# Neighbourhood attention and rotary on one core: bias rows from memory, earlier rotary tables, gate per head

## The chip, the core and the metric

The kernel is one program on one NeuronCore of a Trainium2 chip. TensorE (PE) multiplies matrices and transposes, VectorE (DVE), ScalarE (ACT) and GpSimd (POOL) work element by element, SyncE (SP) issues DMAs, and ACT issues DMAs too, between its own operations. The metric is the device time of one execution in microseconds (us), lower is better. Where the text says head 4, the attention heads are counted from 0.

## The reference, cut to what matters

One layer, 2048 latent tokens on a 32 x 64 grid, 256 context tokens, width 1024:

```python
na_q, na_k, na_v, na_g, r_q, r_k, r_v, r_g = split(rmsnorm_modulated(x) @ w_in)   # and the same for the context
# group A, 8 heads of 64: each query sees an 8 x 16 window of keys, clamped to the grid, and all 256 context keys
s_loc = (q . k_window) * 64**-0.5 + na_rpb[h, dr + 7, dc + 15]     # masked outside of the window
s_ctx = (q . k_ctx) * 64**-0.5
y_na = softmax([s_loc, s_ctx]) @ [v_window, v_ctx] * silu(na_g)
# group B, 4 heads of 128: rotary on r_q and r_k, retention in both directions
y_ret = head_rmsnorm(retention(rotary(r_q), rotary(r_k), r_v)) * silu(r_g)
out = final_rmsnorm(x + gate * (concat(y_na, y_ret) @ w_out))
```

## The kernel before, in words

All matrix products of the projections are made of three terms of a value split into a high and a low part (`hhi`, `hlo` of the activations, `whi`, `wlo` of the weights), so one projection unit is 24 matmuls for 512 columns (`tform`, L351) or 48 for 256 columns (`tokform`, L362). The program has these stages, one after the other in time: preparation and projections up to about 562 us of the span, the attention of group A from 562 to about 1062 us, the rest of the projections and the backward pass of the retention to about 1145 us, and the forward pass of the retention with the output projection to the end. The schedule is manual: every engine executes its instructions in the order in which the Python code emits them.

The attention loop (`for t in range(NT + 3)`, L957) has 16 tiles of 128 queries per head, four row groups `i` of four column tiles `j`, 128 tiles in all. In the pass for tile t it emits the scores of tile t (`s_mm`, PE into PSUM tile `sS`), the normalization of tile t-1 (`s_norm`, L771 on POOL), the pass `s_min` of tile t (L760 on DVE: scores plus a bias row from `nb`, written to `sp`, with the running minimum), the transposes of tile t-2 (`p_tr`, PE, copied by ACT to `pt`, the low part by DVE in `p_lo`), and the product with v of tile t-3 (`pv`), after every second tile `combine`. Between these it calls `fill`, which takes 2 or 3 steps per tile from a generator with the leftover projection units of group B (`u_rv`, `u_rk`, `u_rq`: 8 steps per unit). So PE always has projection matmuls between the attention's own. Engines keep to this order strictly: a DVE instruction of a rotary unit that waits holds back the next `s_min` behind it, and PE cannot write the next `sS` before `s_min` has read the last.

The bias. `s_min` adds a row per query: -(relative position bias) inside the window and a huge number outside of it. The queries are scaled by -0.125, so the sum is the negated score, and the minimum is the softmax's shift. Three row types by three column types of tiles are needed per head. POOL builds the rows (`bias`, L724): from a slab of 16 x 32 values per query (`rpbe`, one load per head) and two small masks it makes `ep` once per row type (L730) and the rows in `nb0` or `nb1` per column type (L733): 12 POOL instructions per head. Edge types 0 and 2 share `nb0`, type 1 has `nb1`.

The loads. SP issues all loads of the stage, in program order: per head the keys `k` (twice 576 KB), the context values `vc`, eight groups of values `vt` of four pieces each (`load_v`, a ring of six groups), the queries `q` of a row group in two halves (`load_q`, a ring of two, asked for when the row group before begins), the gate `gt` (`load_gate`, one buffer), and from `fill` the weights `st`, the activations `hhi`, `hlo` of blocks 2 and 3 that were put aside in memory (`hS`, 16 loads of 512 KB), and the rotary tables. A DMA also waits for the landing of one issued eight or nine places before it in the common order of SP and ACT, whose semaphore it takes over.

Rotary. `u_rq` and `u_rk` load their table inside their own unit (`mid`: after step 3 of 8, or step 2), into the ring `t0` of two buffers, and DVE uses it when the unit's matmuls are done (L412 to L414, L448 and L450), then POOL adds (L415, L451).

The gate. Head pairs share a tile `y2` of 128 partitions: the even head fills partitions 0 to 63, the odd head 64 to 127, and after the odd head's row group POOL multiplies all 128 partitions by `gt` (L825) and ACT stores the tile to `yS`.

Of the kernel before, what the change touches and what calls it, by code (L numbers as in the profile page):

```python
# [18 lines left out]
P = 128  # L19
# [5 lines left out]
GW = 64  # L25
# [11 lines left out]
EROW0 = [4, 0, 0, 0]  # L37
ECOL0 = [8, 0, 0, 0]
# [32 lines left out]
]  # L71
RTYPE = [0, 1, 1, 2]
# [4 lines left out]
def hybrid_kernel(ctx: ExitStack, tc: tile.TileContext, a: dict, out: bass.AP):  # L77
# [290 lines left out]
    def mid(g, n, fn):  # L368
        for m in range(KC):
            next(g)  # L370
            if m == n:
                fn()
            yield
        return (yield from g)

# [24 lines left out]

    def u_rq(w, c0, ct, b):
        def load():
            for key in ("rot_c", "rot_s"):
                rot[key] = op.tile([P, 512], F32, name="t0")
                nc.sync.dma_start(rot[key], a[key][:, b * 512:(b + 1) * 512])

        g = tform(w, ct, b)
        pm, n, tok = yield from mid(g, 3, load) if ct == 0 else g
        rc, rs = rot["rot_c"], rot["rot_s"]
# [22 lines left out]
    def u_rk(w, c0, tp):  # L432
        def load():
            rot["k"] = op.tile([P, 2, 2, P], F32, name="t0")
            nc.sync.dma_start(rot["k"], a["rot_k"][tp * 256:(tp + 1) * 256].rearrange("(t p) s d -> p t s d", p=P))

        g = tokform(w, tp)
        pm = yield from mid(g, 2, load) if tp < 8 else g
        rt = rot.get("k")
# [59 lines left out]
    wseq = [(c0, -0.125 if us[0][0] is u_q else None) for c0, us in jobs[1:]] + [(c0, None) for _, c0 in fseq]  # L499
# [127 lines left out]
    def fill_stream(w):  # L627
# [72 lines left out]
    def load_e(hd, h):  # L700
        hd["e"] = kp.tile([P, 16, 32], F32, name="rpbe", bufs=1)
        nc.sync.dma_start(hd["e"], a["rpb_e"][h])

# [15 lines left out]
    mrow = mp.tile([P, 3, 16], F32, name="mrow")  # L719
    nc.sync.dma_start(mrow, a["na_rows"])  # L720
    mcol = mp.tile([P, 3, 32], F32, name="mcol")
    nc.sync.dma_start(mcol, a["na_cols"])

    def bias(hd, rt, ct):  # L724
        i, j = (0, 1, 3)[rt], (0, 1, 3)[ct]
        kr, cw = KWIN[i][1], CWIN[j][1]
        er, ec = EROW0[i], ECOL0[j]
        if ct == 0:
            hd["ep"] = mp.tile([P, kr, 32], F32, name="ep")
            nc.gpsimd.tensor_tensor(hd["ep"], hd["e"][:, er:er + kr, :],  # L730
                                    mrow[:, rt, er:er + kr].unsqueeze(2).to_broadcast([P, kr, 32]), ALU.subtract)
        t, o = nbz[int(rt == 1)], nbt[int(rt == 1), ct]
        nc.gpsimd.tensor_tensor(t[:, o:o + kr * cw].rearrange("p (a b) -> p a b", b=cw),  # L733
                                mcol[:, ct, ec:ec + cw].unsqueeze(1).to_broadcast([P, kr, cw]),
                                hd["ep"][:, :, ec:ec + cw], ALU.subtract)
# [19 lines left out]
    def s_min(t):  # L755
        h, i, j = dims(t)[:3]
        T = tl_st[t]
        n, big = T["nk"] + LC, int(RTYPE[i] == 1)
        o = nbt[big, CTYPE[j]] - T["lo"]
        nc.vector.tensor_tensor_reduce(T["sp"][:, :n], T["s"], nbz[big][:, o:o + n], 1.0, 3e38, ALU.add, ALU.min, T["st"][:, 0:1])  # L760
# [29 lines left out]
    def pv(t):  # L790
        h, i, j, kr0, kr, kc0, cw = dims(t)
        T, hd = tl_st[t], heads[h]
        pt, ng_, cn = T["pt"], T["ng"], 4 * cw
        if t % 2 == 0:
            tl_st["po"] = psc.tile([P, 2, 2, P], F32, name="po")
        po = tl_st["po"]
        for g in range(ng_):
# [6 lines left out]

    def load_gate(t):
        h, i = dims(t)[:2]
        gts[t // 4] = ap_.tile([P, 512], F32, name="gt", bufs=1)
        nc.sync.dma_start(gts[t // 4], gS[h // 2][:, i * 512:(i + 1) * 512])
# [540 lines left out]
```

## Time and profile before

| | |
|---|---|
| median of 3 runs | 1423.2 us (1421.59 to 1423.46) |
| the profiled execution, its own time | 1420.85 us |
| its span, first to last instruction | 1419.1 us |
| PE busy / DVE / ACT / POOL | 1351.0 / 641.2 / 530.7 / 560.1 us |
| mean granted PE clock | 0.986 |
| DMA, mean | 178 GB/s, 253.19 MB moved |

Times in the profile are counted from the span's start. A busy PE is not a PE at its best rate: the rows of a matmul overlap with the next, and at a lower granted clock (PEclk) the same matmul takes longer. In timeline rows the columns are start, duration, engine, line, operation, output <- inputs, and in brackets the idle time before it on that engine and what ended it. In the queue's rows (SPq) the duration is that of the issue with its wait.

### The profile page before, as it was taken

How to read it: one execution, taken by the hardware profiler on the slowest of the kernel's cores; microseconds unless marked ns; L12 is line 12 of the kernel's file. 1: busy time of each engine (PE TensorE's matmuls, PEld its weight loads, DVE VectorE, ACT ScalarE, POOL GpSimd, SP SyncE). 2: the span in 40 equal slices, each digit the busy share in tenths (PEclk: the TensorE clock that was granted, in tenths of full speed). 3: DMA queues.
4: the chain of work that ended last, by engine and by line, in shares of the span. 5: the costliest groups of instructions: out<-in, count | busy, mean ns of one | idle time of the engine just before them, and what ended most of it. 6: DMA issues, size and time to landing. Idle time of an engine off the chain costs nothing.

```text
span 1419.1 us, 22560 instructions
## 1 busy us (share of the span) xinstructions
PE 1351.0 (95%) x8380; PEld 1181.2 (83%) x8380; DVE 641.2 (45%) x1244; ACT 530.7 (37%) x1155; POOL 560.1 (39%) x579
## 2 busy tenths in 40 slices
PE   6989999999999999999999998898999989999997
PEld 2567899988887887998799888797999879888886
DVE  5786111100021221467766766575663634345445
ACT  5454212212212221555455444354562234333332
POOL 4442302112201221565655644375453155454442
PEclk9999999999999999999999999999999999999999
DMA  9444656223254676556666685757346998555433
GB/s 318 158 164 143 215 207 230 104 97 105 96 157 159 195 276 202 127 156 166 180 157 162 182 243 190 200 153 181 108 125 208 283 297 260 191 170 173 154 120 126
DMA packets 203631, 253.19 MB, mean 178 GB/s; under 512 B 13057, under 2 KB 151425, under 8 KB 202498
## 3 DMA queue, kind: packets, MB, share of 16 engines
q1 hardware_dynamic: 168098, 186.98, 45.2%
q10 hardware_dynamic: 35424, 64.76, 12.5%
q8 instruction: 67, 1.10, 0.3%
q14 instruction: 42, 0.34, 0.1%
HBM read 168.86 MB, written 82.84 MB: 177 GB/s over the span
## 4 chain that ended last, share of the span: by engine, by line
PE 73%; DMA 9%; DVE 6%; issue 3%; POOL 3%; ACT 2%; SPq 2%; DVEq 0%; POOLq 0%; ACTq 0%
PE mm L351 25%; PE mm L362 18%; PE mm L1192 11%; PE sS L751 3%; PE tr L778 2%; PE po L798 2%; PE mm L915 2%; DMA k<-kS 2%; PE tr L780 1%; DMA q<-qS 1%; PE po L800 1%; PE mm L295 1%; PE mm L1104 1%; PE mm L1103 1%; PE mm L1102 1%
## 5 line engine op out<-in xcount | busy, mean ns | idle before, releaser
L351 PE MATMUL mm<-hhi,whi 128*128 128x512 f32 x640 | 260.5, 407 | 0.0
L351 PE MATMUL mm<-hlo,whi 128*128 128x512 f32 x640 | 254.2, 397 | 4.8 <-DVE hlo L264 1.9
L351 PE MATMUL mm<-hhi,wlo 128*128 128x512 f32 x640 | 254.4, 397 | 0.2 <-DVE wlo L332 0.2
L362 PE MATMUL mm<-whi,hhi 128*128 128x256 f32 x768 | 225.5, 294 | 0.0
L362 PE MATMUL mm<-wlo,hhi 128*128 128x256 f32 x768 | 217.7, 283 | 2.5 <-POOL wlo L332 2.5
L362 PE MATMUL mm<-whi,hlo 128*128 128x256 f32 x768 | 217.2, 283 | 0.0
L332 POOL TENSOR_TENSOR wlo<-st,whi 128x256 fp32r<-128x256 f32 (+1 forms) x97 | 111.7, 1171 | 232.7 <-ACT whi L330 232.2
L782 ACT CAST pt<-tr 128x640 fp32r<-128x640 f32 (+1 forms) x128 | 95.6, 747 | 205.4 <-PE tr L780 193.0
L788 DVE TENSOR_TENSOR pt<-tr,pt 128x640 fp32r<-128x640 f32 (+1 forms) x128 | 113.9, 890 | 102.8 <-ACT pt L782 102.1
L362 PEld LDWEIGHTS mm<-wlo,hhi 128*128 128x128 f32 x768 | 146.0, 190 | 3.2 <-POOL wlo L332 3.1
L351 PEld LDWEIGHTS mm<-hlo,whi 128*128 128x128 f32 x640 | 121.4, 190 | 30.1 <-issue 2.5
L362 PEld LDWEIGHTS mm<-whi,hhi 128*128 128x128 f32 x768 | 146.3, 190 | 0.0
L362 PEld LDWEIGHTS mm<-whi,hlo 128*128 128x128 f32 x768 | 146.2, 190 | 0.0
L351 PEld LDWEIGHTS mm<-hhi,wlo 128*128 128x128 f32 x640 | 121.0, 189 | 29.4 <-DVE wlo L332 0.6
L351 PEld LDWEIGHTS mm<-hhi,whi 128*128 128x128 f32 x640 | 121.3, 190 | 28.7 <-issue 4.6
L771 POOL TENSOR_SCALAR sp<-sp,stt 128x640 f32<-128x640 f32 (+2 forms) x128 | 103.4, 809 | 100.7 <-DVE stt L770 79.8
L760 DVE CUSTOM_DVE_ANT_0 sp<-sS,nb 128x640 f32<-128x640 f32 (+2 forms) x128 | 105.5, 825 | 26.4 <-PE sS L751 20.3
L765 ACT ACTIVATE sp<-sp,stt 128x640 f32<-128x640 f32 (+2 forms) x128 | 107.4, 839 | 26.5 <-DVE stt L760 26.0
L751 PE MATMUL sS<-k,q 128*128 128x256 f32 (+3 forms) x512 | 100.6, 319 | 16.9 <-DVE stt L760 13.0
L751 PEld LDWEIGHTS sS<-k,q 128*128 128x128 f32 x512 | 84.5, 191 | 24.4 <-DVE stt L760 15.9
L1192 PE MATMUL mm<-wor,y 128*128 128x512 f32 x384 | 95.4, 397 | 1.0 <-DVE xt L1201 0.9
L1192 PE MATMUL mm<-won,y 128*128 128x512 f32 x336 | 89.9, 406 | 0.0
(216 smaller groups left out, 2307.5 us busy)
## 6 DMA issues: line engine op xcount, KB each, us to landing
st<-in_w_in_dram SPq DMA_DIRECT2D x48, 512.0 KB
q<-qS SPq DMA_DIRECT2D x64, 256.0 KB
vS<-o ACTq DMA_DIRECT2D x18, 512.0 KB
k<-kS SPq DMA_DIRECT2D x16, 576.0 KB
kS<-o SPq DMA_DIRECT2D x16, 512.0 KB
woS<-g ACTq DMA_DIRECT2D x32, 256.0 KB
qS<-o ACTq DMA_DIRECT2D x16, 512.0 KB
vt<-vS SPq DMA_DIRECT2D x128, 64.0 KB
```

The lines of the kernel that those rows point to most:

```text
L332: eng.tensor_tensor(l, r, f(h), ALU.subtract)
L351: nc.tensor.matmul(pm[:, :n], ww[:, k, cs], h[:, k, :], start=(k == 0 and i == 0), stop=(k == KC - 1 and i == 2))
L362: nc.tensor.matmul(pm[:, t * WG:(t + 1) * WG], h[:, k, o:o + P], ww[:, k, :], start=(k == 0 and i == 0), stop=(k == KC - 1 and i == 2))
L751: nc.tensor.matmul(o, hd["q"][i][:, hl, j * P:(j + 1) * P], k, start=(hl == 0), stop=(hl == 1))
L760: nc.vector.tensor_tensor_reduce(T["sp"][:, :n], T["s"], nbz[big][:, o:o + n], 1.0, 3e38, ALU.add, ALU.min, T["st"][:, 0:1])
L765: nc.scalar.activation(sp[:, :n], sp[:, :n], AF.Exp, bias=st[:, 0:1], scale=-1.0, accum_out=st[:, 1:2])
L771: nc.gpsimd.tensor_scalar(sp[:, :n], sp[:, :n], st[:, 2:3], 0.0, ALU.mult, ALU.add)
L778: nc.tensor.transpose(tr[:cn, g, :], sp[:, T["lo"] + g * cn:T["lo"] + (g + 1) * cn], ident)
L782: nc.scalar.copy(pt[:, :ng_ + 2, 0, :], tr[:, :ng_ + 2, :])
L788: nc.vector.tensor_tensor(pt[:, :n, 1, :], tr[:, :n, :], f(pt)[:, :n, 0, :], ALU.subtract)
L798: nc.tensor.matmul(po[:, t % 2, :, :], hd["vt"][kr0 // 4 + g][:cn, j, :], pt[:cn, g, :, :], start=(g == 0), stop=False)
L1192: nc.tensor.matmul(pm, yy[:, k, :], ww[:, k, sl], start=(k == 0 and i == 0), stop=(k == 3 and i == 2))
```

## The change

Four things are changed, and their places in the order of the loop:

- The host lays out the finished rows of bias and mask for each head and each of the nine tile types (`_bias_rows`, 3200 values per query and head, `rpb_t`). `bias` is now one DMA on SP per tile type straight into `nb0` or `nb1`: nine per head, of 128 rows of 288, 384 or 512 values (1152 to 2048 bytes). The slab, the masks, and the 96 POOL instructions are gone.
- The queries are scaled by +0.125, the rows hold the bias itself with a huge negative number outside, and the pass of `s_min` multiplies by -1.0 where it multiplied by 1.0.
- The rotary tables move to a ring of three (`rot` in the pool of `st`) and are asked for at step 2 of the unit before the one that uses them. Where a `u_rq` unit follows a `u_rq` unit, only the first of its two tables is, and the second at the start of its own unit.
- The gate is applied per head: `gt` of 64 partitions is loaded for each row group of every head, at j = 1 instead of j = 3 and into a ring of two, POOL multiplies 64 partitions after each row group (32 multiplications where there were 16), and ACT stores 64 partitions (32 stores where there were 16). The bytes are the same.
- `load_v` asks for value groups 3 and 4 one tile earlier.

```diff
+BT = [[(KWIN[i][1] * CWIN[j][1], 0, 0) for j in (0, 1, 3)] for i in (0, 1, 3)]
...
     def u_rq(w, c0, ct, b):
-        def load():
-            for key in ("rot_c", "rot_s"):
-                rot[key] = op.tile([P, 512], F32, name="t0")
-                nc.sync.dma_start(rot[key], a[key][:, b * 512:(b + 1) * 512])
-        g = tform(w, ct, b)
-        pm, n, tok = yield from mid(g, 3, load) if ct == 0 else g
+        pm, n, tok = yield from tform(w, ct, b)
+        rc, rs = rot["rot_c", b], rot["rot_s", b]
...
         def steps(g):
-            for v in g:
+            n = at[0]
+            at[0] += 1
+            is_rq = lambda k: k >= 0 and order[k][0] is u_rq
+            if is_rq(n - 1):
+                for e in needs(n)[1:]:
+                    rot_load(*e)
+            for m, v in enumerate(g):
+                if m == 2:
+                    for e in needs(n + 1)[:1 if is_rq(n) else 2]:
+                        rot_load(*e)
...
-    def bias(hd, rt, ct):
-        i, j = (0, 1, 3)[rt], (0, 1, 3)[ct]
-        kr, cw = KWIN[i][1], CWIN[j][1]
-        er, ec = EROW0[i], ECOL0[j]
-        if ct == 0:
-            hd["ep"] = mp.tile([P, kr, 32], F32, name="ep")
-            nc.gpsimd.tensor_tensor(hd["ep"], hd["e"][:, er:er + kr, :],
-                                    mrow[:, rt, er:er + kr].unsqueeze(2).to_broadcast([P, kr, 32]), ALU.subtract)
-        t, o = nbz[int(rt == 1)], nbt[int(rt == 1), ct]
-        nc.gpsimd.tensor_tensor(t[:, o:o + kr * cw].rearrange("p (a b) -> p a b", b=cw),
-                                mcol[:, ct, ec:ec + cw].unsqueeze(1).to_broadcast([P, kr, cw]),
-                                hd["ep"][:, :, ec:ec + cw], ALU.subtract)
+    def bias(h, rt, ct):
+        n, o = BT[rt][ct]
+        nc.sync.dma_start(nbz[int(rt == 1)][:, nbt[int(rt == 1), ct]:][:, :n], a["rpb_t"][h, :, o:o + n])
...
-        nc.vector.tensor_tensor_reduce(T["sp"][:, :n], T["s"], nbz[big][:, o:o + n], 1.0, 3e38, ALU.add, ALU.min, T["st"][:, 0:1])
+        nc.vector.tensor_tensor_reduce(T["sp"][:, :n], T["s"], nbz[big][:, o:o + n], -1.0, 3e38, ALU.add, ALU.min, T["st"][:, 0:1])
...
-        if h % 2 == 1 and jp == 1:
-            gt, y2 = gts.pop(t // 4), ys[i]
-            nc.gpsimd.tensor_tensor(y2, y2, gt, ALU.mult)
-            y_put(h // 2, i // 2, (i % 2) * 512, y2, 2)
+        if jp == 1:
+            gt = gts.pop(t // 4)
+            nc.gpsimd.tensor_tensor(y2[fin], y2[fin], gt[fin], ALU.mult)
+            store(yS[i // 2][h // 2, fin, (i % 2) * 512:(i % 2) * 512 + 512], y2[fin], 2)
...
-        if h % 2 == 1 and j == 3:
+        if j == 1:
             load_gate(t)
...
-        for g in {(0, 3): (3,), (1, 0): (4,), (1, 1): (5,), (1, 3): (6,), (2, 3): (7,)}.get((i, j), ()):
+        for g in {(0, 2): (3,), (0, 3): (4,), (1, 1): (5,), (1, 3): (6,), (2, 3): (7,)}.get((i, j), ()):
...
                 if j == 0:
                     load_q(nh, h + 1, 0)
-                    bias(nh, 0, 0)
+                    bias(h + 1, 0, 0)
                     load_v(nh, (0,))
```

PE's and DVE's instructions keep their order and number. Three places show what moves.

POOL, first tiles of head 0 (`wlo` is the low part of weights that the leftover units use, `sp` the scores of a tile, L771 their normalization), before:

```order
L332 TENSOR_TENSOR wlo<-st,whi 128x256 x2
L730 TENSOR_TENSOR ep<-rpbe,mrow 128x512
L733 TENSOR_TENSOR nb_3987<-mcol,ep 128x384
L771 TENSOR_SCALAR sp<-sp,stt 128x544
L332 TENSOR_TENSOR wlo<-st,whi 128x256 x2
L733 TENSOR_TENSOR nb_3987<-mcol,ep 128x512
L771 TENSOR_SCALAR sp<-sp,stt 128x640
```

The same place in the changed kernel, where the normalization is L768:

```order
L336 TENSOR_TENSOR wlo<-st,whi 128x256 x2
L768 TENSOR_SCALAR sp<-sp,stt 128x544
L336 TENSOR_TENSOR wlo<-st,whi 128x256 x2
L768 TENSOR_SCALAR sp<-sp,stt 128x640
L336 TENSOR_TENSOR wlo<-st,whi 128x256 x3
```

The two bias instructions that stood ahead of each first normalization of a row type are gone.

SP, head 4, from the end of its first reload of `hS` to the queries of its row group 3 (the `q` in the last row but one of the first list), before:

```order
L684 DMA hhi<-hS_0_85 128x1024
L435 DMA t_7514<-in_rot_k_dram 128x2x256
L684 DMA hlo<-hS_1_86 128x1024
L694 DMA k_7532<-kS_63 64x2304 x2
L697 DMA vc<-vS_66 128x2x128
L716 DMA vt<-vS_66 96x1x128
L716 DMA vt<-vS_66 128x1x128 x2
L716 DMA vt<-vS_66 96x1x128
L708 DMA q<-qS_59 64x1024 x2
L702 DMA rpbe<-in_rpb_e_dram 128x512
```

The same place in the changed kernel:

```order
L699 DMA hhi<-hS_0_85 128x1024
L403 DMA rot<-in_rot_c_dram 128x512
L403 DMA rot<-in_rot_s_dram 128x512
L699 DMA hlo<-hS_1_86 128x1024
L709 DMA k_7539<-kS_63 64x2304 x2
L712 DMA vc<-vS_66 128x2x128
L727 DMA vt<-vS_66 96x1x128
L727 DMA vt<-vS_66 128x1x128 x2
L727 DMA vt<-vS_66 96x1x128
L732 DMA nb_3984<-in_rpb_t_dram 128x288
L719 DMA q<-qS_59 64x1024 x2
```

Ahead of these queries now stand two rotary tables where one stood, and a bias row.

SP, head 5, around the queries of its row group 3 (last row of the first list), before:

```order
L694 DMA k_8269<-kS_64 64x2304 x2
L697 DMA vc<-vS_66 128x2x128
L405 DMA t_8285<-in_rot_c_dram 128x512
L405 DMA t_8287<-in_rot_s_dram 128x512
L808 DMA gt<-gS_69 128x512
L716 DMA vt<-vS_66 96x1x128
L716 DMA vt<-vS_66 128x1x128 x2
L716 DMA vt<-vS_66 96x1x128
L708 DMA q<-qS_59 64x1024 x2
```

In the changed kernel, from the tables on:

```order
L403 DMA rot<-in_rot_c_dram 128x512
L403 DMA rot<-in_rot_s_dram 128x512
L727 DMA vt<-vS_66 96x1x128
L727 DMA vt<-vS_66 128x1x128 x2
L727 DMA vt<-vS_66 96x1x128
L699 DMA hlo<-hS_1_88 128x1024
L719 DMA q<-qS_59 64x1024 x2
L809 DMA gt<-gS_69 64x512
L727 DMA vt<-vS_66 96x1x128
L727 DMA vt<-vS_66 128x1x128 x2
L727 DMA vt<-vS_66 96x1x128
L709 DMA k_8282<-kS_64 64x2304 x2
```

The tables moved ahead of the keys, past a reload, the queries of row group 2, the gate and two groups of values.

More of the change, by code (lines that the diff above doesn't have):

```diff
@@ L71 @@
 ]
+BT = [[(KWIN[i][1] * CWIN[j][1], 0, 0) for j in (0, 1, 3)] for i in (0, 1, 3)]
+BN = 0
+for _row in BT:
+    for _c in range(3):
+        _row[_c] = (_row[_c][0], BN)
+        BN += _row[_c][0]
 RTYPE = [0, 1, 1, 2]
@@ L366, in tokform @@
         return pm
[L368 to L374, printed above, removed]
     def u_k(w, c0, ct, b):
@@ L432, in u_rk @@
     def u_rk(w, c0, tp):
[L433 to L439, printed above, removed]
+        pm = yield from tokform(w, tp)
+        rt = rot["rot_k", tp].rearrange("p (t s d) -> p t s d", t=2, s=2) if tp < 8 else None
         o = op.tile([P, 2, 2, WG], F32, name="o")
@@ L796, in pv @@
         po = tl_st["po"]
+        cn = 4 * cw
         for g in range(ng_):
@@ L812, in combine @@
         po, jp = tl_st["po"], j // 2
[L813 to L816 removed]
+        fin, oth = fin_(h), fin_(h + 1)
+        if jp == 0:
+            ys[i] = ap_.tile([P, 512], F32, name="y2", bufs=2)
+        y2 = ys[i]
         tmp = ap_.tile([P, 2, P], F32, name="cmb", bufs=1)
@@ L834, in hybrid_kernel @@
     heads[0] = load_head(0)
-    load_e(heads[0], 0)
     load_q(heads[0], 0, 0)
@@ L841, in hybrid_kernel @@
             for ct in range(3):
-                bias(heads[0], 0, ct)
+                bias(0, 0, ct)
     NT = 16 * NH
@@ L999, in hybrid_kernel @@
                 heads[h + 1] = load_head(h + 1)
-            if i == 2 and j == 1:
-                load_e(heads[h + 1], h + 1)
             if i == 3:
```

91 lines of the change are left out of this document (48 added, 43 removed).

## The prediction

> **What bounds the kernel now.** I read the page's head, then busy time in the attention stage and in its last eighth, then PE's waits there.
>
> ```profile
> span 1419.1 us, 22560 instructions
> ...
> 561.00:1065.00 504.00, 473.57 (x3505) 447.60 (x3504) 323.31 (x723) 260.09 (x544) 281.53 (x323) 0.97 0.61 166
> 1002.00:1065.00 63.00, 63.00 (x525) 62.60 (x524) 39.71 (x89) 36.45 (x75) 32.24 (x38) 1.00 0.42 118
> ```
>
> The columns after the length are PE, PEld, DVE, ACT and POOL busy, the granted clock, the DMA share and GB/s. Everything that the change touches, but a few rotary loads, runs in these 504 us. PE is the bound there: in the last eighth it is never idle, and 525 matmuls in 63 us make 8.33 per us. DVE, ACT and POOL are busy for 52 to 64% of the stage, so less work on POOL is worth nothing by itself. What can be won is the 30.4 us in which PE is idle (504 less 473.57) and the slow clock that follows a gap. PE's waits in the stage:
>
> ```profile
> PE sS L751 <- DVE stt L760: 13.0, 7, 6.6
> PE tr L778 <- POOL sp L771: 10.3, 7, 4.5
> PE sS L751 <- DMA q<-qS: 3.6, 1, 3.6
> ```
>
> These three (total, times, longest) are nearly all of it, and each is in reach of one part of the change. I took them one by one in the timeline.
>
> **Part 1, the bias leaves POOL.** The rows of the work that goes and of the work behind it:
>
> ```profile
> L733 POOL TENSOR_TENSOR nb<-mcol,ep 128x288 f32<-128x288 f32 (+2 forms) x72 | 68.7, 955 | 3.9 <-DVE stt L760 2.0
> L730 POOL TENSOR_TENSOR ep<-rpbe,mrow 128x384 f32<-128x384 f32 (+1 forms) x24 | 21.8, 907 | 11.6 <-DMA rpbe<-in_rpb_e_dram 11.6
> L825 POOL TENSOR_TENSOR y<-y,gt 128x512 f32<-128x512 f32 x16 | 20.7, 1291 | 44.5 <-DVE y L821 44.5
> ```
>
> 90.5 us leave POOL. They count only where a bias instruction stands between a tile's reciprocal and its normalization L771, and PE then waits for L771 with its transposes. Three such places:
>
> ```profile
> 567.89 1.05 POOL L730 TENSOR_TENSOR ep<-rpbe,mrow 128x512 f32<-128x512 f32 x1
> 569.03 1.01 POOL L733 TENSOR_TENSOR nb<-mcol,ep 128x384 f32<-128x384 f32 x1
> 570.01 0.73 POOL L771 TENSOR_SCALAR sp<-sp,stt 128x544 f32<-128x544 f32 x1
> 570.79 0.88 PE L778 MATMUL tr<-ident,sp 128*96 128x128 f32 x3 [1.35 <-POOL sp L771]
> ...
> 630.77 1.05 POOL L730 TENSOR_TENSOR ep<-rpbe,mrow 128x512 f32<-128x512 f32 x1
> 631.90 0.99 POOL L733 TENSOR_TENSOR nb<-mcol,ep 128x384 f32<-128x384 f32 x1
> 633.65 0.53 PE L778 MATMUL tr<-ident,sp 128*96 128x128 f32 x3 [1.78 <-POOL sp L771]
> ...
> 983.22 1.00 POOL L733 TENSOR_TENSOR nb<-mcol,ep 128x384 f32<-128x384 f32 x1
> 985.15 1.11 PE L778 MATMUL tr<-ident,sp 128*128 128x128 f32 x4 [4.54 <-POOL sp L771]
> ```
>
> At 570 the normalization could start at the end of the reciprocal, about 1 us sooner: 1.0 of 1.35 goes. At 633 2.1 us of bias go, more than the gap: 1.78. At 985, where weights were late, 1.0 of 4.54. Two more:
>
> ```profile
> 670.15 0.79 POOL L733 TENSOR_TENSOR nb<-mcol,ep 128x288 f32<-128x288 f32 x1
> 671.88 0.66 PE L778 MATMUL tr<-ident,sp 128*128 128x128 f32 x4 [1.49 <-POOL sp L771]
> ...
> 686.18 1.02 POOL L733 TENSOR_TENSOR nb<-mcol,ep 128x384 f32<-128x384 f32 x1
> 688.03 0.55 PE L778 MATMUL tr<-ident,sp 128*128 128x128 f32 x3 [0.69 <-POOL sp L771]
> ```
>
> They give 0.8 and 0.7. Sum: 5.3 us off (0.7 to 6.1, if other work moves into the places).
>
> The clock after the gap at 570, and after two gaps of part 2:
>
> ```profile
> 570.00:576.80 6.80, 6.01 (x28) 5.99 (x29) 1.72 (x4) 2.42 (x6) 6.80 (x10) 0.50 0.25 77
> 843.00:846.50 3.50, 3.27 (x9) 2.30 (x10) 2.18 (x6) 1.03 (x2) 3.42 (x5) 0.51 0.93 211
> 911.30:918.10 6.80, 2.91 (x8) 2.29 (x9) 4.94 (x9) 1.03 (x2) 3.13 (x3) 0.50 0.70 164
> ```
>
> In 6.8 us at half clock PE did 28 matmuls, worth 3.4 us at 8.33 per us; 0.8 of the lost 3.4 is the gap itself, so the clock cost 2.6. I take 2.5 off, since the gap that set it off shrinks to a quarter (bounds 0 and 3.4). The Trainium skill, TensorE: Matmul & The Clock Gate, section Why this matters for your kernels, says that a drop needs an idle gap of about 3 us or more between bursts of matmuls. The trace does not agree: the gap at 570 was 1.35 us, and the clock was 0.50. By the page the 2.5 us would not belong to this gap, and the time below would be 2.5 higher, 1416.5.
>
> **Part 2, rotary tables one unit ahead.** The chain of waits and the timeline at the late tables:
>
> ```profile
> 840.83 0.42 DVE L448 TENSOR_TENSOR o<-mm,t 128x256 f32<-128x256 f32 x1 [2.92 <-DMA t<-in_rot_k_dram]
> 843.23 1.65 PE L751 MATMUL sS<-k,q 128*128 128x512 f32 x4 [2.70 <-DVE stt L760]
> ...
> 903.60 8.46 DMA t<-in_rot_s_dram
> 912.15 0.69 DVE L412 TENSOR_TENSOR o<-mm,t 64x512 f32<-64x512 f32 x1 [5.92 <-DMA t<-in_rot_s_dram]
> 915.19 1.65 PE L751 MATMUL sS<-k,q 128*128 128x512 f32 x4 [6.55 <-DVE stt L760]
> ```
>
> DVE waits for a table, the next `s_min` stands behind it, and PE behind that. The tile pace is
>
> ```profile
> L751 PE MATMUL sS<-k,q x512: 274/291/795, 561.9 to 1058.5; 128*128 128x256 f32 x86, 128*128 128x384 f32 x44, 128*128 128x512 f32 x21, 128*128 128x288 f32 x20
> ```
>
> 496.6 us over 127 tiles, 3.9 us. The loop's 131 passes take 318 steps of the leftover units, 2.4 per tile, so a request that is 8 or 9 steps earlier (step 2 of the unit before, instead of step 2 or 3 of its own) comes 13 to 14 us earlier, against 5.92 and 2.92 of lateness. Both DVE waits go. At 912 that is 6.55 us, and with the slow clock, in which 8 matmuls (1 us) took the last 2.9 us, about 8 off. What is late next there is the queries of row group 3. They are issued now at
>
> ```profile
> 911.98 1.13 SPq L708 DMA_DIRECT2D q<-qS  x2
> 924.15 0.67 PE L751 MATMUL sS<-k,q 128*128 128x288 f32 x4
> ```
>
> and PE would want them at 916 instead of 924. The tables and a gate no longer stand between the keys and them, a bias row does; I leave 2 us of wait: 6 off (0 to 8).
>
> At 843 it is 2.70 and about 1.7 of clock, 4.4. But the next wait is already there:
>
> ```profile
> 835.03 13.75 DMA k<-kS
> 848.80 7.27 DMA q<-qS
> 856.20 0.82 PE L751 MATMUL sS<-k,q 128*128 128x288 f32 x4 [3.65 <-DMA q<-qS]
> ```
>
> The queries of head 4's row group 3 wait for the landing of the keys, in a backlog of reloads; PE's progress doesn't move them. PE arrives 4.4 us sooner and waits 4.4 us longer: 0 (0 to 4.4 off).
>
> **Part 3, the new transfers.** Per head 3200 values x 128 queries x 4 bytes are 1.64 MB, 13.1 MB in all, for 2.1 MB of slabs: 11 MB more, and 78 more DMAs on SP.
>
> ```profile
> q1 hardware_dynamic: 168098, 186.98, 45.2%
> ```
>
> 45.2% of the span for 186.98 MB is 3.4 us per MB, so 38 us of service in a stage whose DMA share goes from 0.61 to about 0.68. On average that is hidden; in heads 4 and 5 (reloads) it is not. Ahead of the queries above come half a gate (0.13 MB), one more table (0.26) and a bias row (0.15): 1.9 us, so PE's wait grows by 2 (0 to 5). Behind `s_min` of tiles 12, 14 and 15 of each head SP now waits for DVE, with the next head's values and queries queued behind; the bias row itself is needed three tiles (11.7 us) later, and the slowest small load above took 8.46. I put 1 us (0 to 6) for queries with little slack. The Trainium skill, DMA: Bandwidth & Descriptors, section Anatomy of one DMA, gives 2.0 us plus bytes at 436 GB/s, for the path issued by GpSimd, as an estimate 2.6 us for a table of 256 KB; the trace has 8.46 on SP's path under load. By the page every load of part 3 would be hidden and the time 3 us lower, 1411.
>
> **Part 4, the gate.** 16 more multiplications of 1.3 us on POOL (the partitions halve, the row length doesn't). Among the 16 of the odd heads two are in the rows above that precede a gap, some 0.7 us each: 1.5 more (0 to 3). The additional stores are issues on ACT, which has 48% of the stage idle: 0. What SP waited for the single gate buffer goes:
>
> ```profile
> SPq L808 <- POOL y L825: 76.5, 11, 10.3
> ```
>
> No wait of PE ends there now: 0. Scale and sign of `s_min`, the earlier value groups: 0, the same instructions on DVE, and PE never waits for `vt`.
>
> **The sum.** -5.3 - 2.5 - 6 + 0 + 2 + 1 + 1.5 = -9.3 us, against the profiled execution's own 1420.85: 1411.6. That execution is 2.4 under the median of the runs, 1423.2; on the median it is 1414. Within 0.2%, 2.8 us, a measurement of this kernel can't tell a change.
>
> **Rivals.** (a) Slower: SP's queue becomes the bound. The place is the load of queries: at head 6, row group 1, the issue and the need are
>
> ```profile
> 945.41 1.13 SPq L708 DMA_DIRECT2D q<-qS  x2
> 953.16 0.86 PE L751 MATMUL sS<-k,q 128*128 128x384 f32 x4 [0.16 <-DVE stt L760]
> ```
>
> 6.6 us from the end of the issue, while 7.27 was seen. With three waits for DVE and nine bias rows per head ahead, queries that are 2 us late cost those and 1.5 of slow clock. At five places that is 17.5 us on top of 1414: 1431. It decides from 9.3 us, three such places. Against it: SP loses 76.5 us of waits for the gate. (b) Better: freed of these waits, SP runs ahead, the queries of head 4 and 5 come in time, and nothing of parts 2 and 3 is given back: -5.3 - 2.5 - 8 - 4.4 + 1.5 = -18.7, 1404.5. Against it: the 13.75 us of the keys are a backlog of bytes. (c) No change: the wait for the table is filled by late queries (0 for -6), and transfers cost 5 instead of 3: about -1.3, 1422.
>
> **Chances.** Forecast 0.45, (a) 0.20, (b) 0.20, (c) 0.15. The forecast's own range is 1408 to 1420, nearly all of it faster; (b) too. Faster 0.63, same 0.17, slower 0.20. The range from 1403 to 1430 takes in (b) and (c) and most of (a).
>
> **What would show it.** Right: no wait for `rot` at L412 or L448 (new lines), PE's waits for POOL in the stage halved to some 5 us, of them 3.5 at the late weights; PE's wait for `q` grows from 3.6 to about 10 us, at head 4. Granted clock 1.00 around 570. Wrong: new waits of PE for `q` or of DVE for `nb` in most heads (a), or no wait for `q` at all (b).

## The result: 0.5% slower, and the profile after

| | before | after |
|---|---|---|
| median of 9 runs each, us | 1421.65 | 1430.26 |
| after / before | | 1.0054, 95% interval 1.0033 to 1.0076 |
| span of the profiled execution, us | 1419.1 | 1430.0 |

The prediction was 1414 (1403 to 1430), faster. The change made the kernel slower by 0.33 to 0.76%, so the case that came is that of rival (a), 1431 us. From here on, line numbers are those of the kernel named; in the changed kernel `s_mm` is L748, `s_min` L757, `s_norm` L768, the transposes L775, `p_lo` L785, `pv` L796, the bias rows' load L732, the queries' L719, the values' L727, the gate's L809.

The same views as those shown ahead of the result, now of the changed kernel. All views are of one execution each; that of the changed kernel took 1431.96 us, that of the kernel before 1420.85. First the whole and the attention stage (length, PE, PEld, DVE, ACT, POOL busy, granted clock, DMA share, GB/s):

```profile
span 1430.0 us, 22693 instructions
...
561.00:1079.00 518.00, 475.73 (x3500) 448.53 (x3499) 322.69 (x722) 260.12 (x544) 218.86 (x247) 0.97 0.69 184
1016.00:1079.00 63.00, 62.33 (x514) 61.54 (x513) 38.39 (x86) 36.24 (x75) 26.12 (x31) 1.00 0.48 133
...
q1 hardware_dynamic: 177282, 197.93, 48.1%
```

The stage takes 518 us in place of 504 for about the same 3500 matmuls. PE's idle time in it grew from 30.4 to 42.3 us (518 less 475.73), its busy time by 2.2. POOL is 63 us less busy, and the DMA share went from 0.61 to 0.69 with the 10.95 MB that the queue carries more (197.93 less 186.98). What comes behind the stage took 351 us in place of 354, which gave 3 of the 14 us back in this execution.

PE's waits in the stage, and DVE's one wait for a bias row:

```profile
PE sS L748 <- DMA q<-qS: 21.8, 7, 6.6
PE po L796 <- DMA vt<-vS: 7.0, 2, 3.9
PE tr L775 <- DVE pt L785: 4.7, 5, 1.9
PE sS L748 <- DVE stt L757: 3.5, 5, 1.0
PE tr L775 <- POOL sp L768: 0.4, 1, 0.4
...
DVE sp L757 <- DMA nb<-in_rpb_t_dram: 1.2, 1, 1.2
```

The two waits that the change was aimed at are gone: POOL from 10.3 to 0.4 us, DVE from 13.0 to 3.5 with no wait for a table. In their place stand queries, 3.6 before and 21.8 now, and values, which never came late before. Of these 28.8 us, 22.8 lie in heads 4 and 5: queries 3.96, 5.31 and 6.59 us late (PE goes on at 836.95, 864.07 and 920.08) and both late values. Rows of the clock at 570 and at the three longest slow stretches:

```profile
570.00:576.80 6.80, 6.80 (x59) 6.80 (x59) 3.92 (x9) 4.80 (x12) 4.20 (x6) 1.00 0.51 134
835.00:842.00 7.00, 5.05 (x23) 5.08 (x24) 1.05 (x3) 1.05 (x2) 0.00 (x0) 0.51 0.77 210
858.90:869.20 10.30, 5.13 (x18) 4.48 (x19) 1.19 (x3) 1.29 (x2) 0.00 (x0) 0.50 0.81 192
913.50:923.80 10.30, 3.72 (x14) 3.36 (x14) 0.83 (x2) 0.00 (x0) 0.00 (x0) 0.50 0.78 212
```

The first row is the stretch that ran at 0.50 before and is at 1.00 now, with 59 matmuls in place of 28. The other three lie in heads 4 and 5, behind late queries and late values; before, there was slow clock there at 843 to 846, 857 to 860 and 911 to 918. Outside of these heads the stage has two more slow stretches now, at 705 and 999, and had two before, at 570 and 983. In all, PE had half its clock for 34.1 us of the stage now and for 27.3 before.

SP's waits in the stage, and the row of before for the values:

```profile
SPq L732 <- DVE stt L757: 46.0, 19, 5.2
SPq L173 <- POOL wlo L336: 22.9, 9, 6.5
SPq L727 <- DMA vt<-vS: 22.7, 30, 2.5
SPq L727 <- DMA q<-qS: 11.1, 20, 1.5
...
SPq L716 <- DMA vt<-vS: 13.1, 20, 1.4
```

The wait for the gate's buffer (76.5 before) is all but gone (1.1), one for `s_min` of 46.0 stands in its place, and waits for the landing of other loads are longer and more frequent (values 13.1 in 20 before, 22.7 in 30 now).

One of the two worst places is head 4, row group 3. The chain of waits there (start, length, what; pieces under 0.1 us left out):

```profile
845.54 1.30 POOL o L444
846.87 10.57 DMA rkS<-o
857.45 0.33 SPq L732
857.89 0.49 SPq L719
858.42 5.51 DMA q<-qS
863.93 0.14 issue
864.07 1.24 PE sS L748 x4
```

Read from below: PE starts its scores when the queries have landed. They were only 5.51 us on their way, less than the 7.27 of before; what is late is their issue, at 857.89 in place of 846.42, while PE came to these scores at 858.76 in place of 852.55. SP stood at a bias row just ahead of them, and that waited for the landing of a store of rotated keys, 10.57 us, which ACT's queue had requested and which has nothing to do with either. The program gives the transfers of SP's and ACT's queues eight semaphores in turn, and an issue waits until the transfer that had its semaphore last has landed. Before, the landing of the keys, 13.75 us, stood in that place, and the store of rotated keys one further on, where the slab (`rpbe`) waited 1.5 us for it. So the change also shifted which transfer waits for which.

### The profile page after: what moved, and what is told of

It is laid out like the page before. It is cut to its first block, busy times and chain, and to the rows that moved or that the text cites. A ratio compares the mean times of both kernels' runs of the same rounds, so it can differ in the third digit from the quotient of the medians.

```text
span 1430.0 us, 22693 instructions
## 1 busy us (share of the span) xinstructions
PE 1351.1 (94%) x8380; PEld 1179.9 (83%) x8380; DVE 641.0 (45%) x1244; ACT 531.0 (37%) x1155; POOL 495.0 (35%) x499
## 3 DMA queue, kind: packets, MB, share of 16 engines
q1 hardware_dynamic: 177282, 197.93, 48.1%
## 4 chain that ended last, share of the span: by engine, by line
PE 73%; DMA 13%; DVE 7%; issue 2%; ACT 2%; POOL 2%; SPq 1%; ACTq 0%; DVEq 0%; POOLq 0%
PE mm L355 25%; PE mm L366 18%; PE mm L1190 10%; DMA q<-qS 5%; PE sS L748 4%; PE tr L775 2%; PE po L796 2%; DMA vt<-vS 2%; PE mm L915 2%; PE mm L299 2%; PE tr L777 1%; PE po L798 1%; DMA v<-rvS 1%; PE mm L1102 1%; PE mm L1101 1%
## 5 line engine op out<-in xcount | busy, mean ns | idle before, releaser
L785 DVE TENSOR_TENSOR pt<-tr,pt 128x640 fp32r<-128x640 f32 (+1 forms) x128 | 113.9, 890 | 105.2 <-ACT pt L779 104.6
L768 POOL TENSOR_SCALAR sp<-sp,stt 128x640 f32<-128x640 f32 (+2 forms) x128 | 103.7, 811 | 136.0 <-DVE stt L767 94.9
L757 DVE CUSTOM_DVE_ANT_0 sp<-sS,nb 128x640 f32<-128x640 f32 (+2 forms) x128 | 105.6, 825 | 53.4 <-PE sS L748 43.0
L748 PE MATMUL sS<-k,q 128*128 128x256 f32 (+3 forms) x512 | 101.7, 321 | 27.3 <-DMA q<-qS 21.8
L748 PEld LDWEIGHTS sS<-k,q 128*128 128x128 f32 x512 | 85.1, 192 | 36.5 <-issue 19.9
```

Of the source, the lines that this page charges most:

```text
L748: nc.tensor.matmul(o, hd["q"][i][:, hl, j * P:(j + 1) * P], k, start=(hl == 0), stop=(hl == 1))
L768: nc.gpsimd.tensor_scalar(sp[:, :n], sp[:, :n], st[:, 2:3], 0.0, ALU.mult, ALU.add)
L785: nc.vector.tensor_tensor(pt[:, :n, 1, :], tr[:, :n, :], f(pt)[:, :n, 0, :], ALU.subtract)
```

## Experiments

All ratios are to runs of the kernel before on the same chip, with 95% intervals; a difference of ratios is turned into us with 1422 us. Waits are from one profiled execution of each kernel. The diffs show the lines that matter; `...` stands for what is left out. Theory Q puts the loss on SP's order and its waits, B on the bytes of the bias rows, R on the earlier rotary requests. Two kernels' difference is uncertain by some 3.5 us.

### One part undone or alone

The changed kernel with the rotary requests back in their own unit:

```diff
-            for m, v in enumerate(g):
-                if m == 2:
-                    for e in needs(n + 1)[:1 if is_rq(n) else 2]:
-                        rot_load(*e)
+            for v in g:
...
+        pm, n, tok = yield from mid(g, 3, load) if ct == 0 else g
...
+        pm = yield from mid(g, 2, load) if tp < 8 else g
```

> The changed kernel with the rotary tables requested as before (inside their own unit); bias rows by DMA and gate per head stay. Theory Q (SP's queue: the queries stand behind bias rows that wait for DVE and behind more DMAs): the loss stays and the waits of DVE for tables come back, 1431 to 1437 us, PE's wait for q still near 20 us. Theory B (the 11 MB of bias rows load the DMA engines in heads 4 and 5): the same, 1431 to 1437. Theory R (the earlier requests fall into the reloads and push the queries back): the loss goes, 1416 to 1423, PE's wait for q back to about 4 us.

Measured: 1435.75 us, 1.0092 (1.0073 to 1.0111). R is out: the earlier requests do not cost, they gain 5.4 us (uncertain by 4.1). DVE's wait for the key tables is back, and PE behind it:

```profile
PE sS L737 <- DVE stt L746: 18.4, 7, 7.2
PE sS L737 <- DMA q<-qS: 10.7, 5, 4.1
...
DVE o L452 <- DMA t<-in_rot_k_dram: 10.7, 3, 5.7
```

The kernel before with the bias part alone:

```diff
-            nc.gpsimd.tensor_tensor(hd["ep"], hd["e"][:, er:er + kr, :],
...
-        nc.gpsimd.tensor_tensor(t[:, o:o + kr * cw].rearrange("p (a b) -> p a b", b=cw),
...
+        nc.sync.dma_start(nbz[int(rt == 1)][:, nbt[int(rt == 1), ct]:][:, :n], a["rpb_t"][h, :, o:o + n])
```

> The kernel before with the bias part alone: rows laid out by the host and loaded by SP, negation inside the bias pass; rotary tables and gate as before. Theories Q and B: the loss is here, 1428 us or more, since the waits for POOL that go (10 us) are given back as waits for q. Theory R, or that the gate per head does it: this alone gives 1413 to 1417 (5.3 and 2.5 us off 1421.7).

Measured: 1435.68 us, 1.0101 (1.0081 to 1.0121). The loss is here, 14.4 us. PE's wait for queries is only 7.6 us in it; PE waits 25.2 us for DVE, which waits for a key table:

```profile
PE sS L737 <- DVE stt L746: 25.2, 8, 9.4
PE sS L737 <- DMA q<-qS: 7.6, 6, 2.9
...
DVE o L452 <- DMA t<-in_rot_k_dram: 11.8, 3, 7.5
```

So a loss of this size shows here as late tables and in the changed kernel, where the tables are asked for earlier, as late queries.

The kernel before with the gate part alone, with and without the earlier value groups:

```diff
-        if h % 2 == 1 and j == 3:
+        if j == 1:
             load_gate(t)
...
-        if h % 2 == 1 and jp == 1:
...
-            nc.gpsimd.tensor_tensor(y2, y2, gt, ALU.mult)
...
+        if jp == 1:
...
+            nc.gpsimd.tensor_tensor(y2[fin], y2[fin], gt[fin], ALU.mult)
...
-        for g in {(0, 3): (3,), (1, 0): (4,), ...
+        for g in {(0, 2): (3,), (0, 3): (4,), ...
```

> The kernel before with the gate per head alone (gate loads of half the partitions in every head, 16 more multiplications, 16 more stores) and value groups 3 and 4 requested one tile earlier. The prediction's part 4: 1.5 us more, 1422 to 1425. If SP's waits for the gate buffer had cost something: 1415 to 1419. If the additional transfers are a part of the loss: 1427 or more.

Measured: 1431.35 us, 1.0059 (1.0042 to 1.0076), 8.4 us more, over five times what the prediction put (1.5). PE's wait for POOL grew as the prediction said, from 10.3 us by 4.3, about half of the loss:

```profile
PE tr L778 <- POOL sp L771: 14.6, 15, 3.2
```

> The kernel before with the gate per head, value groups 3 and 4 requested where they were. The gate part with the earlier value groups took 8.6 us more than the kernel before (ratio 1.0059). If the earlier value groups do it (SP waits for PE to free their buffers, with the queries of row group 2 behind): 1420 to 1425. If the gate itself does it (16 more multiplications ahead of normalizations, or SP freed from its waits and running ahead): 1428 to 1434.

Measured: 1427.97 us, 1.0053 (1.0036 to 1.0069), 7.5 us more than before: most of the loss stays, so the value groups are not its main part. The same edit in the changed kernel:

```diff
-        for g in {(0, 2): (3,), (0, 3): (4,), ...
+        for g in {(0, 3): (3,), (1, 0): (4,), ...
```

> The changed kernel with value groups 3 and 4 requested where they were before. If the earlier value groups cost 5 us or more: 1421 to 1425. If they cost nothing here, where SP runs late anyway (9.9 us of waits for their buffers in the changed kernel): 1428 to 1432.

Measured: 1426.7 us, 1.0043 (1.0027 to 1.0059), between the two expectations and not to be told from the changed kernel.

The changed kernel without its gate part (the diff of the gate part, reversed):

> The changed kernel without its gate part: bias rows by DMA and rotary tables one unit ahead, the gate per pair of heads and the value groups as before. The gate part alone cost 6 to 8.6 us on the kernel before. If it costs the same here: 1421 to 1425. If its cost lay in POOL's work before normalizations, which the bias part takes away: within 3 us of the changed kernel, 1427 to 1432. If its freeing SP from the wait for the gate buffer helped here: 1434 or more.

Measured: 1424.75 us, 1.0025 (1.0010 to 1.0040): the gate part costs 4.1 us (0.4 to 7.8) in the changed kernel. Without it, the rotary part is worth 10.8 us (1.0101 of the bias part alone to 1.0025).

Only the 16 additional multiplications taken away:

```diff
+            if h % 2 == 1:
                 nc.gpsimd.tensor_tensor(y2[fin], y2[fin], gt[fin], ALU.mult)
```

> The changed kernel without the multiplication by the gate in the even heads (their outputs stay ungated); gate loads and stores of every head stay. Taking the whole gate part out gave 5.5 us. If the 16 additional multiplications on POOL (1.3 us each, ahead of normalizations) are its cost: 1424 to 1426. If the 16 additional loads and stores and SP's order are: 1429 to 1432.

Measured: 1428.0 us, 1.0035 (1.0018 to 1.0052), 2.7 us less than the changed kernel, uncertain by 3.9: it does not decide between the multiplications and the transfers.

### Bytes against order

Same requests in the same order, but 64 bytes per partition in seven heads, whose bias this kernel leaves out:

```diff
         n, o = BT[rt][ct]
+        n = n if h == 0 else 16
```

> The changed kernel, but for heads 1 to 7 each bias row's transfer brings only its first 16 columns (64 bytes per partition in place of 1152 to 2048), so the bias of these heads is left out; the number of DMAs, their order and their waits are the same. About 10.9 MB fewer are moved. Theory B: the loss goes with the bytes, 1414 to 1420, PE's wait for q under 8 us. Theory Q: within 3 us of the changed kernel, 1427 to 1432, PE's wait for q 18 us or more.

Measured: 1417.14 us, 0.9966 (0.9952 to 0.9979), faster than before. That is B's number: 12.5 us (9 to 16) go with 10.96 MB. But the rest of B's expectation failed: PE still waits 15.7 us for queries, and SP still 45.2 for DVE.

```profile
PE sS L749 <- DMA q<-qS: 15.7, 4, 6.1
...
SPq L733 <- DVE stt L758: 45.2, 19, 5.2
...
839.56 10.92 DMA rkS<-o
850.49 0.33 SPq L733
850.93 0.49 SPq L719
851.47 4.21 DMA q<-qS
```

The chain at head 4's row group 3 has the same links as in the changed kernel, and the landing of the store takes as long (10.92 us, 10.57 there): these late queries are not the bytes' doing. Late queries and values in heads 4 and 5 come to 18.7 us here and to 22.8 there. The bytes show along the whole stage instead: the changed kernel's scores start 5.6 us after those of the short rows at head 4 (804.89 and 799.31), 11.5 at head 6 (953.46 and 941.92) and 16.8 at the last tile (1072.50 and 1055.66), in two executions that are 16.6 us apart.

Short rows in the bias part alone (the same line, added there):

> The bias part alone, but for heads 1 to 7 each bias row's transfer brings only its first 16 columns (the bias of these heads is left out). The bias part alone took 13 us more than before (1435.7). If the bytes are all of its loss, as short rows in the changed kernel suggest (13.1 us): 1413 to 1423, at or below the kernel before by the 5 to 8 us of POOL waits. If SP's waits for DVE and the 78 more requests cost as much as the bytes: 1427 to 1432.

Measured: 1424.3 us, 1.0023 (1.0006 to 1.0039): 11.1 us less than with full rows, so the price of the bytes is about the same with and without the other parts. The waits for POOL are gone here, without a gain in time, since DVE is later for its tables (13.0 us before):

```profile
PE sS L738 <- DVE stt L747: 21.8, 9, 8.1
PE tr L765 <- POOL sp L758: 0.7, 1, 0.7
```

Short rows in heads 4 and 5 alone, beside the reloads (`n = 16 if h in (4, 5) else n`):

> The changed kernel, but for heads 4 and 5 alone each bias row's transfer brings only its first 16 columns (the bias of these two heads is left out). 3.1 MB fewer are moved, all next to the reloads. Short rows in heads 1 to 7 gave 13.1 us. If the bytes cost only beside the reloads, as the prediction put it: 10 us or more, 1416 to 1421. If they cost in every head alike: two sevenths, 3.8 us, 1425 to 1428.

Measured: 1426.14 us, 1.0028 (1.0013 to 1.0043), 3.7 us (0 to 7.4) less than the changed kernel. Two sevenths of 12.5 are 3.6, as if the bytes cost in every head alike; 10 us beside the reloads are excluded. Against short rows in seven heads this kernel is 8.8 us slower (6 to 12), so the bytes of the other five heads have a price too. PE's waits for queries stay (14.6 us, 21.8 in the changed kernel).

The rows requested by POOL, so that SP neither issues them nor waits for DVE ahead of them:

```diff
-        nc.sync.dma_start(nbz[...
+        nc.gpsimd.dma_start(nbz[...
```

> The changed kernel with the 72 bias rows requested by POOL in place of SP: same bytes, same places in the program, but SP neither issues them nor waits for DVE ahead of them. Theory Q: 1414 to 1421, PE's wait for q under 10 us. Theory B: within 3 us of the changed kernel, 1427 to 1433. Either: if issuing costs POOL more than about 1 us each, PE's waits for POOL rise above the 0.4 us of the changed kernel and the difference is put to that.

Measured: 1428.72 us, 1.0046 (1.0029 to 1.0062), as B said, 1.1 us less than the changed kernel (uncertain by 3.8). Late queries are fewer, but PE's waits for POOL took some of it back (0.4 before the edit), as the last sentence of the expectation allowed:

```profile
PE sS L748 <- DMA q<-qS: 12.6, 3, 6.5
PE po L796 <- DMA vt<-vS: 8.3, 1, 8.3
PE tr L775 <- POOL sp L768: 5.8, 8, 1.9
```

If these 5.4 us are set against it, SP's waits for DVE are worth some 6.5 us (uncertain by 3.8 for the noise alone), half of what the bytes are worth. The rows also left the turn of eight semaphores here: SP waits for the landing of a bias row seven times in the changed kernel (3.3 us) and never in this one. That alone did not free the queue: its wait for DVE gave way to 70.4 us for the values' buffers.

### Loads earlier, or spread

Queries one row group earlier, in three buffers, with the gate in one buffer and later:

```diff
-        q = kp.tile([P, 2, 512], F32R, name="q", bufs=2)
+        q = kp.tile([P, 2, 512], F32R, name="q", bufs=3)
...
-        gts[t // 4] = ap_.tile([P, 512], F32, name="gt", bufs=2)
+        gts[t // 4] = ap_.tile([P, 512], F32, name="gt", bufs=1)
...
-        if j == 1:
+        if j == 3:
             load_gate(t)
-        if i < 3 and j == 0:
-            load_q(hd, h, i + 1)
+        if i < 2 and j == 0:
+            load_q(hd, h, i + 2)
+        if i == 2 and j == 0 and h + 1 < NH:
+            load_q(heads[h + 1], h + 1, 0)
+        if i == 3 and j == 0 and h + 1 < NH:
+            load_q(heads[h + 1], h + 1, 1)
...
```

> The changed kernel with three buffers for queries, each requested one row group (four tiles, 15.6 us) earlier; to fit, the gate has one buffer and is requested two tiles later. Bytes and bias rows as in the changed kernel. Theory L (the bytes cost only through late queries): PE's wait for q falls from 21.8 us to under 4, the waits for vt stay near 7, and the time is 1413 to 1420. Theory B in its strong form (whatever is earlier, the loads as a whole are late in heads 4 and 5): the wait moves to vt and to DVE's tables, 1426 to 1431.

Measured: 1424.99 us, 1.0016 (0.9996 to 1.0036), 5.4 us less (uncertain by 4.2), where 21.8 us of waits for queries went. None is left among PE's waits, but the next loads in the queue are late instead:

```profile
PE po L796 <- DMA vt<-vS: 11.2, 2, 8.2
...
DVE sp L757 <- DMA nb<-in_rpb_t_dram: 14.7, 5, 7.9
```

With value group 6 ahead of the next head's keys as well (`(1, 3): (6,)` becomes `(1, 2): (6,)`):

> As the one with three buffers for queries, and in addition value group 6 of each head is requested one tile earlier, ahead of the next head's keys. Theory L: PE's waits for vt (7.0 us in the changed kernel) go too, with the slow clock behind them: 2 to 7 us below the kernel with early queries alone, 1408 to 1415. If the keys then come too late or DVE's tables do: within 2 us of it.

Measured: 1427.47 us, 1.0041 (1.0023 to 1.0059). It met neither expectation: PE's waits for values fell to 3.0 us, but one for POOL of 11.1 us and longer waits for bias rows (16.6) came.

The reloads of activations spread over three times as many steps:

```diff
-        dmas.extend([None] * 3)
         for k in range(0, KC, 2):
             for hl in range(2):
+                dmas.extend([None] * 2)
                 dmas.append(...hS[b - 2][hl]...)
```

> The changed kernel with the two reloads of activations (4 MB each, 8 transfers of 512 KB) issued one per three steps of the leftover units in place of one per step, so over 24 steps (10 tiles, 40 us) in place of 8 (13 us). Theory S (the bias rows' bytes cost where the DMA engines are already full, and SP, with eight transfers under way at most, stands behind the reload): the two late queries of heads 4 and 5 and the slow clock behind them go, 1416 to 1422. Theory E (the bytes cost in every head alike, the reload is only where PE's waits show): within 3 us of the changed kernel, 1427 to 1432.

> The kernel before with the reloads spread in the same way. Theory S: the waits around 843 and 857 and at 912 shrink here too, 4 to 10 us off: 1412 to 1418. Theory E, or that late tables are set by SP's order: 1420 to 1424. Together with the changed kernel's spread: if both gain the same, the bias rows' loss is elsewhere.

Measured: changed kernel 1425.64 us, 1.0025 (1.0012 to 1.0039); kernel before 1418.79 us, 0.9981 (0.9963 to 0.9999). Both lie between what theories S and E expected, so neither is confirmed. They gain 4.1 and 2.7 us, less than theory S asks for, and the distance between the two kernels is 6.3 us (3.1 to 9.5) where it was 7.7: most of the loss stays when the reloads are spread. The kernel before with spread reloads is the only one with all of the computation whose whole interval lies below the kernel before, by a hair.

Spread reloads and early queries, on the changed kernel:

> The changed kernel with spread reloads and with queries requested one row group earlier (three buffers; the gate with one buffer, two tiles later). Early queries alone gave 1425.0. Theory S: both causes of late loads gone, 1408 to 1416, faster than before. Theory E: at or above 1422, with waits for bias rows, tables or values in place of those for queries.

Measured: 1420.97 us, 0.9996 (0.9979 to 1.0013). These edits (the gate with one buffer among them, as with early queries alone) give back the loss, 8.2 us (uncertain by 3.9), and no more; what is late now are bias rows:

```profile
DVE sp L757 <- DMA nb<-in_rpb_t_dram: 24.3, 6, 10.5
```

Spread reloads without the gate part:

> The changed kernel with spread reloads and without its gate part (gate and value groups as before): bias rows by DMA, rotary tables one unit ahead. Spread alone gave 4.7 us, taking the gate part out 5.5. If these are separate costs: 1419 to 1422, at the kernel before. If both lift the same wait for queries in heads 4 and 5: 1423 to 1426.

Measured: 1423.75 us, 1.0015 (0.9996 to 1.0034), 5.5 us below the changed kernel. Spread alone gave 4.1, the gate part taken out alone 4.1. The measured 5.5 is less than their sum, as if both lifted the same waits, but it is uncertain by 4.1, so this is not shown.

Last, the bias back on POOL, with the other two parts kept (the gate with one buffer, `bufs=1`, requested at `j == 3`, which makes room for the tables):

> The changed kernel without its bias part: bias computed on POOL as before; rotary tables one unit ahead and gate per head stay, the gate with one buffer requested in tile 3 as before, the value groups where they were. If the bias rows' transfers are the loss, and the gate costs what the prediction put (1.5 us): before less 6 plus 1.5, 1415 to 1421, no wait of DVE for tables. If the gate's 16 more multiplications on POOL beside the bias cost 8 us: 1422 to 1428.

Measured: 1439.76 us, 1.0129 (1.0107 to 1.0151), the slowest of all and far outside both expectations. SP waits for the single gate buffer 24 times, with queries and values behind it:

```profile
SPq L823 <- POOL y L840: 123.2, 24, 10.9
...
PE tr L789 <- POOL sp L782: 13.5, 12, 4.9
PE sS L762 <- DMA q<-qS: 11.3, 5, 4.2
PE po L810 <- DMA vt<-vS: 10.4, 2, 6.8
```

So this kernel says nothing clean of the bias part. It shows a held queue, but such a wait is not a loss by itself: with early queries SP waited 72.1 us for the same buffer in a kernel 16 us faster. How much of the 18.3 us is the one buffer and how much the gate's work beside the bias on POOL was not separated.

## Why the prediction was wrong

**Part 1, right in the waits, and paid back elsewhere.** PE's waits for POOL went from 10.3 to 0.4 us (5 were expected to stay), and the slow clock at 570 went. The prediction put that drop down to the gap of 1.35 us alone and passed over another of 1.52 us that ended at 567.88, where DVE's pass was late. Now the first gap and the drop are gone and the second is down to 1.02 us, so the 2.5 us that the rule of the Trainium skill, TensorE: Matmul & The Clock Gate, section Why this matters for your kernels, would have left out were rightly counted. But with the bytes taken out, the bias part alone is still 3.3 us (0.9 to 5.5) slower than before, where -5.3 - 2.5 were put: PE waits 21.8 us for DVE in place of 13.0, and DVE 9.2 us for a key table in place of 2.9.

**Part 2, right.** -6 was predicted, and 5.4 us were gained beside the gate part (uncertain by 4.1), 10.8 without it. No wait for a table is left. That head 4's row group 3 has late queries anyway was right, only more so: 5.31 us of wait where 3.65 was.

**Part 3, the step that failed.** Its terms were 2 and 1 us. Short rows put the bytes at 12.5 us (9 to 16). The prediction had the 38 us of service "on average hidden" at a share of 0.68 and costing only in heads 4 and 5. The share was foretold well (0.69), the conclusion was not. PE's long waits for loads do lie in heads 4 and 5, but most of them stay when the bytes go (18.7 of 22.8 us), and the price of the bytes is spread over the stage: 3.7 us for heads 4 and 5, 8.8 for the other five. For the late queries it counted only the bytes of what stands ahead of them. The chain shows another cause: SP's next issue waits for the landing of an earlier transfer of either queue. By which path the bytes cost is not shown. That they lengthen landings, and landings hold the issues, is likely: SP's waits for landings in the stage were 57.6 us before, 119.8 in the changed kernel and 98.6 with short rows. But the landing followed in the chain did not shorten with the bytes.

**Part 4, mis-sized.** 1.5 us (0 to 3) was put, 4.1 measured in the changed kernel and 7.5 to 8.4 alone. Half of the multiplications gone gave 2.7, which can't be told from 0 or from 4.1. That nothing is won when the gate's wait of 76.5 us goes was right.

**The sum.** With 12.5 for 3 and 4.1 for 1.5, -9.3 becomes +2.8; measured are +7.7 (4.7 to 10.8). The 5 us that are left (uncertain by some 4) are of the size of what earlier queries give (5.4), and queries were late with short rows too (15.7 us). That this is the missing term is possible, not shown, since the terms do not add: the bias part alone costs 14.4, the gate part alone 8.4, the two together 13.1.

**The rivals.** (a) had the symptom and the time: it counted on five late queries and 1431, and there were seven and 1430.3. That the time fits so closely is in part luck. Its example, head 6, row group 1, was 1.44 us late, and three queries in heads 4 and 5 make 15.9 of the 21.8 us. Its mechanism, SP's waits for DVE, is the smaller half by the rows requested by POOL, and 45.2 us of these waits stayed with the short rows, which were fast. The one argument against it, that SP loses 76.5 us of waits, was no argument, as the gate part alone shows. (b) and (c) put the transfers at 0 and 5 us and failed at the same step. By the Trainium skill, DMA: Bandwidth & Descriptors, section Anatomy of one DMA, every load would have been hidden: its 2.0 us plus bytes at 436 GB/s, for the path issued by GpSimd, make 2.6 us for 256 KB as an estimate. The queries above, on SP's path, took 5.51, a store of the same size on ACT's 10.57. The trace does not agree on these paths under this load.

Open: which of the gate part's loads, stores and multiplications costs what, by which path the bytes cost, and whether more semaphores for all transfers would free the queue. None was settled; taking the bias rows alone out of the turn (requested by POOL) gave 1.1 us.

## What to carry to other kernels

Work on an engine that was idle for 44% of the stage was replaced by 11 MB of loads, and they were not hidden although the DMA share was only 0.6 to 0.7: here they cost 1.1 us per MB (0.8 to 1.5), a third of their 3.4 us per MB of service, and not only beside the reloads. Before a load is called hidden, look at what the queue's next issue waits for (here the landing of unrelated transfers), and price the delay of everything behind it. Take parts apart in pairs, not only one by one: in this stage, where one queue issues all loads, the gains and losses of the parts do not add, and earlier queries handed most of their lateness to the next loads.

## Of the hardware, not expected

In the changed kernel's trace the length of a gap in PE does not tell whether the clock drops. PE's timeline at two places (start, length of the group, idle time before it in brackets):

```profile
666.23 0.73 PE L748 MATMUL sS<-k,q 128*128 128x288 f32 x4 [2.87 <-DMA q<-qS]
666.80 0.39 PE L355 MATMUL mm<-hhi,whi 128*128 128x512 f32 x1
...
705.30 0.96 PE L796 MATMUL po<-pt,vt 128*128 128x256 f32 x3 [1.49 <-DVE stt L767]
706.48 0.63 PE L355 MATMUL mm<-hhi,whi 128*128 128x512 f32 x1
```

After a gap of 2.87 us a matmul of 512 columns took 0.39 us; after one of 1.49 it took 0.63, and the clock from 705.32 to 708.73 was 0.50. The gap of about 3 us that the Trainium skill, TensorE: Matmul & The Clock Gate, section Why this matters for your kernels, gives for a drop agrees with the first place and not with the second.

What the traces do show is a grid. The ten slow stretches of the stage, five before and five after, last 3.41, 6.83 or 10.24 us, and within each trace their starts are whole multiples of 3.41 us apart (changed kernel: 705.32, 835.02, 858.92, 913.53, 998.86). Busy times in cells of this grid, two around the first place, the one ahead of the second, and the one ahead of the drop at 570 in the kernel before:

```profile
660.95:664.36 3.41, 2.24 (x15) 1.59 (x13) 3.17 (x9) 1.92 (x5) 2.85 (x3) 1.00 1.03 190
664.36:667.78 3.42, 1.55 (x10) 1.40 (x11) 0.80 (x3) 0.21 (x1) 3.32 (x5) 1.00 0.43 111
701.91:705.32 3.41, 1.44 (x9) 1.03 (x9) 3.32 (x8) 1.36 (x4) 0.86 (x1) 1.00 0.93 219
...
566.57:569.98 3.41, 1.56 (x10) 1.35 (x10) 1.85 (x6) 2.40 (x8) 2.69 (x3) 1.00 0.40 145
```

The long gap is divided between two cells, and no drop follows; the short one lies in one cell that holds other gaps too, with 1.44 us of PE work in it, and a drop follows. So idle time is better counted per cell than per gap. It does not settle the matter: 1.55 us of work led to no drop and 1.56 to one. What else decides, no run here shows.
